# Separate row tiles, single-bank value products and a shorter hand order in the gating and memory attention of a decoder layer

## The chip, the cores and the metric

The kernel runs on one core of a Trainium2 chip. The metric is the device time of one execution in microseconds (us). A core has TensorE (PE in the profile; PEld are its weight loads), VectorE (DVE), ScalarE (ACT), GpSimd (POOL), and SyncE (SP), which issues the DMA transfers. Each engine works through its own queue in order.

## The reference

One layer of a decoder trunk on `x` of 1024 positions by 1024 channels: a half-step SwiGLU, a projection `z` with three gated branches, an output projection, a second half-step SwiGLU. What the change touches are branch A, the chunked spatial gating, and branch C, attention into 256 memory tokens:

```python
z = rmsnorm(x, mix_norm) @ w_in          # columns u, v, c_q, c_kv, k_rope, q_mem, gates
u = gelu(z[..., U]); v = gelu(z[..., V])
# A: 8 chunks of 128 positions, 8 groups of 64 channels
v = layernorm(v, ln_g, ln_b).reshape(B, nc, CHUNK, SG_GROUPS, SG_GROUP_DIM)
mixed = einsum('gts,bcsgd->bctgd', tril(w_s), v) + b_s
y_a = u * mixed.reshape(B, S, SG_WIDTH)
# C: 4 heads of 128, 256 memory tokens
q = rmsnorm(q_mem); kv = rmsnorm(mem, mem_norm) @ w_kv; k = rmsnorm(kv[K]); v = kv[V]
y_c = softmax(q @ k.T * MD ** -0.5) @ v
merged = sum(sigmoid(gate_i) * (y_i @ W_branch_i) for i in A, B, C)
```

## The kernel before, in words

Every product is computed to float32 accuracy from two halves of each operand: `split` (L129 to L131) makes `hi` by a cast on ScalarE (L130) and `lo = x - hi` on VectorE (L131); `split_gain` does the same with a factor (L139, L140); `mm3` (L144 to L150) issues three matmuls, hi·hi (L147), lo·hi or hi·lo (L148, L149). PSUM tiles come from four single banks (`bank`, 512 columns each) and from two tiles of two banks (`mm`).

After the first SwiGLU and the projections, `mixer` (L1005) calls `sgu` (L614), which does branch A's mixing and, in the same stretch, all of the memory attention:

- `take(hf)` for both halves of 512 positions. `gelu_rows` multiplies and applies gelu (L601) to four chunks of 128 positions by 512 channels, into `rows`. VectorE takes the statistics (L643, L644), normalises (L647, L649), and a split gives `v_hi`, `v_lo` (L130, L131). `take(0)` and `take(1)` run parts of `mem_norm`, the norm of the memory rows, between their products.
- `mix(hf)` does eight groups of three matmuls, one group to a bank. ScalarE evicts each group with its bias into `m` (L661). After a `yield` it transposes `m` (L668) and multiplies by `u` (L669), and splits the result.
- In the tile pool of `sgu`, `rows` (L636) and `m` (L656) have the same name "u" and one buffer: both halves' rows and both halves' `m` follow each other in it.
- `mem_kv` makes the memory keys and values. Its first product is followed by `head_norm` (L697 Square, L698 copy, L699 sum) and by mix(0)'s matmuls; in the middle of its second product stand mix(0)'s transposes. Key transposes (L425) follow. `mem_queries` squares the query columns on ScalarE (L784, out of `raw`, in two halves of 64 rows), adds on GpSimd (L787), splits the queries, and sums with a `pick` matrix (L794).
- `branches(0, ...)` is branch A's projection, a generator of steps of 12 matmuls each.
- `mem_attention` interleaves, for eight blocks of 128 queries: `scores` (S: products into an `mm` tile, minimum L816, factor L817, exponentials L821, division L825 and L826), `turn` (T: eight transposes L863 into banks and splits), `value` (V: products for two blocks and a split), and steps of branch A (F). A table in the code gives the sequence.

From `mem_kv` to the end of `mem_attention`, the lines stand in a `manual_schedule` block for TensorE: TensorE issues in the order in which the code is written. Outside such a block the tile framework's scheduler chooses the order of each engine. The other engines are always in the scheduler's order. Afterwards follow branch C's projection (`branch_pairs`), the latent attention B, its projection, the output projection and the second SwiGLU.

Of the kernel before, what the change touches and what calls it, by code (L numbers as in the profile page):

```python
# [8 lines left out]
F32 = mybir.dt.float32  # L9
# [7 lines left out]
P = 128  # L17
# [6 lines left out]
SGW = 512  # L24
# [8 lines left out]
MH = 4  # L33
MD = 128
# [11 lines left out]
class Kernel:  # L46
# [551 lines left out]
    def gelu_rows(self, dst, h, w, pairs, amid={}):  # L598


        gelu = lambda d, x: self.nc.scalar.activation(d, x, ACT.Gelu)  # L601
        ps = [self.mm() for _ in range(2)] if pairs else [self.bank() for _ in range(4)]
        for d in range(DT):
            then = amid[d]() if d in amid else None
            for i in range(4):
                b = ps[i // 2][:, i % 2] if pairs else ps[i]
                first = self.mm3(b, tuple(x[:, i * P:(i + 1) * P] for x in h[d]), w[d], d == 0, d == DT - 1)
                if then:
                    self.after(first, then)
                then = None  # L610
        for i, b in enumerate(ps):
            gelu(dst[:, 2 * i:2 * i + 2] if pairs else dst[:, i], b)

    def sgu(self, h, p, sink):  # L614
        nc, a, tc = self.nc, self.a, self.tc
        v8 = lambda tag, dt=F32R: p.tile([P, 4, SGW], dt, name=tag, tag=tag, bufs=2)
        if True:
            ln_g = self.bcast_row(p, "ln_g", a["sg_ln_g"], SGW)
            ln_b = self.bcast_row(p, "ln_b", a["sg_ln_b"], SGW)
            ws = self.raw().rearrange("p (g t) -> p g t", g=SGG)  # L620
            nc.sync.dma_start(ws, a["sg_w"])
            nc.gpsimd.affine_select(
                out=ws, in_=ws, compare_op=ALU.is_ge, fill=0.0, base=0,
                pattern=[[0, SGG], [1, P]], channel_multiplier=-1,
            )
            whi, wlo = (x.rearrange("p (g t) -> p g t", g=SGG) for x in self.split_pair())
            self.split(whi, wlo, ws)
            mem = self.mem_norm()
            next(mem)
            w = self.load(a["w_v"])  # L630
            vs, yt = [], []

            def take(hf, amid={}):
                vhi, vlo = (v8(n) for n in ("v_hi", "v_lo"))
                vs.append((vhi, vlo))
                rows = p.tile([P, 4, SGW], F32, name="u")  # L636
                self.gelu_rows(rows, h[hf], w, hf == 0, amid)
                for i in range(0, 4, 2):
                    st = self.small.tile([P, 2, 6], F32, name="bn", tag="bn")
                    mv = self.small.tile([P, 2, 2], F32, name="mv", tag="mv")  # L640
                    v = rows[:, i:i + 2]
                    for k in range(2):
                        nc.vector.bn_stats(st[:, k], v[:, k])  # L643
                        nc.vector.bn_aggr(mv[:, k], st[:, k])  # L644
                    r = self.rms(mv[:, :, 1], 2, 1)
                    for k in range(2):
                        nc.vector.scalar_tensor_tensor(  # L647
                            v[:, k], in0=v[:, k], scalar=mv[:, k, 0:1], in1=ln_g, op0=ALU.subtract, op1=ALU.mult)
                        nc.vector.scalar_tensor_tensor(  # L649
                            v[:, k], in0=v[:, k], scalar=r[:, k:k + 1], in1=ln_b, op0=ALU.mult, op1=ALU.add)  # L650
                    self.split(vhi[:, i:i + 2], vlo[:, i:i + 2], v)

            def mix(hf):
                if not yt:
                    yt.extend(self.split_pair() for _ in range(4))
                m, v = p.tile([P, 4, SGW], F32, name="u"), vs[hf]  # L656
                for g in range(SGG):
                    b = self.bank()[:, :4 * SGW // SGG].rearrange("p (c d) -> p c d", c=4)
                    cols = slice(g * SGW // SGG, (g + 1) * SGW // SGG)
                    self.mm3(b, (whi[:, g], wlo[:, g]), tuple(x[:, :, cols] for x in v), True, True)  # L660
                    nc.scalar.activation(m[:, :, cols], b, ACT.Identity, bias=self.sg_b[:, g:g + 1])  # L661
                yield
                for j in range(4):
                    u = self.row()
                    nc.sync.dma_start(u, self.z[ZU + j][:, hf])
                    b = self.bank()
                    for c in range(4):
                        nc.tensor.transpose(b[:, c * P:(c + 1) * P], m[:, c, j * P:(j + 1) * P], self.ident)  # L668
                    nc.vector.tensor_tensor(u, u, b, op=ALU.mult)  # L669
                    self.split(*(t[:, hf * 512:hf * 512 + 512] for t in yt[j]), u)  # L670

            take(0, {7: lambda: next(mem)})
            take(1, {3: lambda: next(mem)})
            m0, m1 = mix(0), mix(1)
            with tc.manual_schedule(engines={mybir.EngineType.PE}):
                kv = self.mem_kv(next(mem), (lambda: next(m0, None), lambda: next(m0, None)))
                rooms = [v8(n).rearrange("p (a b) w -> p a (b w)", a=2) for n in ("v_hi", "v_lo")]
                queries = self.mem_queries([(x[:, 0], x[:, 1]) for x in rooms])
                next(queries)
                next(m1)  # L680
                rooms = [v8(n, F32) for n in ("v_hi", "v_lo")]
                rooms = [x.rearrange("p (a h) (b m) -> p a (h b) m", a=2, b=2)[:, k] for x in rooms for k in range(2)]
                branch = self.branches(0, yt, sink)
                next(branch)
                next(m1, None)
                yc = self.mem_attention(next(queries), rooms, *kv, branch)
        return yc

    def head_norm(self, x, ps):
# [15 lines left out]
    def mem_norm(self):  # L705


        nc, a = self.nc, self.a
        views = lambda n, dt: [t[:, i].rearrange("p (c m) -> p c m", m=ML)[:, c]
                               for t in (self.h4(dt) for _ in range(n)) for i in range(2) for c in range(2)]  # L710
        x4 = [self.x4() for _ in range(2)]
        x = [t[:, i, c * ML:(c + 1) * ML] for t in x4 for i in range(2) for c in range(2)]
        for n, t in enumerate(x4):
            nc.sync.dma_start(
                t.rearrange("p a (b m) -> p (a b) m", b=2), a["mem"][:, 4 * n:4 * n + 4])
        acc = self.row()[:, :2 * ML].rearrange("p (a m) -> p a m", a=2)
        for n, t in enumerate(x4):
            sq = self.x4() if n == 0 else sq2
            nc.scalar.activation(sq, t, ACT.Square)
            if n == 0:  # L720
                first, sq2 = sq, self.x4()
        nc.vector.tensor_tensor(first, first, sq2, op=ALU.add)
        nc.vector.tensor_tensor(acc, first[:, 0].rearrange("p (a m) -> p a m", a=2),
                                first[:, 1].rearrange("p (a m) -> p a m", a=2), op=ALU.add)
        nc.vector.tensor_tensor(acc[:, 0], acc[:, 0], acc[:, 1], op=ALU.add)
        yield
        ss = self.token_sums(acc[:, 0], late=True)
        last = self.final
        r = self.rms(ss, ML // P, D)
        yield last  # L730
        scale = self.norm_scale(r, late=True, bank=lambda: self.mm()[:, 0])
        last = self.final
        hi, lo = views(2, F32R), views(2, F32R)
        for c in range(DT):
            self.norm_put(hi[c], lo[c], x[c], self.g_mem[:, c:c + 1], scale)
        yield last
        yield hi, lo
# [63 lines left out]
    def mem_attention(self, queries, rooms, kt, vv, filler):  # L801
# [35 lines left out]

        def value(i):
            pt = st.pop(i)
            o = self.mm().rearrange("p a (b q) -> p (a b) q", b=2)  # L840
            for hh in range(MH):
                for m in range(2):
                    s = tuple(t[:, m, hh * MD:(hh + 1) * MD] for t in vv)
                    self.mm3(o[:, hh], s, tuple(t[:, hh] for t in pt[m]), m == 0, m == 1)
            for hh in range(MH):
                self.split(*(t[:, 2 * i * P:2 * (i + 1) * P] for t in yt[hh]), o[:, hh])

        S, T, V = scores, turn, value
        F = lambda: next(filler, None)
        yt = [self.split_pair(self.h4) for _ in range(MH)]  # L850
# [1152 lines left out]
```

## Time and profile before

| | us |
|---|---|
| median of 3 runs (2221.55 to 2222.67) | 2222.58 |
| the profiled execution | 2222.69 |
| its span, first to last instruction | 2221.0 |
| TensorE busy | 2180.9 (98%) |
| VectorE busy | 1564.4 (70%) |
| ScalarE busy | 912.7 (41%) |

The profile comes from one execution. Each timeline row has the start, the duration, the engine, the line, the operation, and out<-in by tile names; a bracket at its end tells how long the engine stood idle before it, and whose result ended this. A wait of TensorE for a tile is named after what was last released for it. A matmul's shown duration is longer than the distance to the next start, since they are pipelined; the spacing of starts is what a matmul costs. Window rows give the busy time of each engine within a stretch, and the mean clock that TensorE was granted there (1.00 is full).

The stretch of the change: `take(1)`'s last matmuls end at 1124 us, mix(0) starts at 1135.0, mix(1) at 1166.3, the first turn at 1200.4, and the last value ends at 1256.3.

### The profile page before, as it was taken

What the parts mean: (1) busy time and instruction counts of PE and PEld (TensorE: products, weight loads), DVE (VectorE), ACT (ScalarE), POOL (GpSimd) and SP (SyncE); (2) the same over time, 40 slices, a digit from 0 to 9 for tenths busy, and PEclk for the clock granted to TensorE, in tenths of its full rate; (3) what the DMA queues carried; (4) which work ended last, traced back from release to release, by engine and by line L of the source; (5) the groups of instructions that cost most, each with busy time, mean ns of one, the idle gap of its engine ahead of it and who ended that gap; (6) DMA issues with size and microseconds to landing.
All of it is one profiled execution on the core that took longest, in us unless ns stands there. A gap on an engine that the chain in (4) does not pass through costs nothing. (4 is left out here: it accounts for less than half of the span.)

```text
span 2221.0 us, 27576 instructions
## 1 busy us (share of the span) xinstructions
PE 2180.9 (98%) x10256; PEld 1818.3 (82%) x10256; DVE 1564.4 (70%) x2402; ACT 912.7 (41%) x1507; POOL 249.0 (11%) x252
## 2 busy tenths in 40 slices
PE   9999999999999999999979999999999999999999
PEld 5788888888887888888767889988888888888887
DVE  7966666579888555545887668895886666657884
ACT  5422222243455333344465448843342222224432
POOL 0012111100000000001300131140002121210000
PEclk9999999999999999999989999999999999999999
DMA  4242323484432333331634550085033333328543
GB/s 144 81 147 95 101 101 108 152 308 149 150 109 95 115 104 114 133 102 42 224 105 166 213 209 30 30 286 201 35 104 110 100 114 100 114 99 301 179 128 104
DMA packets 116085, 294.29 MB, mean 133 GB/s; under 512 B 13680, under 2 KB 22000, under 8 KB 115952
## 3 DMA queue, kind: packets, MB, share of 16 engines
q1 hardware_dynamic: 115952, 292.55, 38.4%
q8 instruction: 80, 1.31, 0.2%
q14 instruction: 53, 0.43, 0.1%
HBM read 206.00 MB, written 86.51 MB: 132 GB/s over the span
## 5 line engine op out<-in xcount | busy, mean ns | idle before, releaser
L135 ACT CAST whi<-x 128x1024 fp32r<-128x1024 f32 (+1 forms) x201 | 191.2, 954 | 501.8 <-PE one L148 220.3
L1345 DVE TENSOR_TENSOR t<-t,one 128x512 f32<-128x512 f32 x186 | 127.8, 687 | 243.6 <-PE one L149 242.8
L147 PE MATMUL bank<-h,whi 128*128 128x512 f32 x676 | 263.3, 390 | 0.0
L148 PE MATMUL bank<-h,whi 128*128 128x512 f32 x676 | 263.1, 389 | 0.0
L149 PE MATMUL bank<-h,wlo 128*128 128x512 f32 x676 | 263.0, 389 | 0.0
L136 DVE TENSOR_TENSOR wlo<-x,whi 128x1024 fp32r<-128x1024 f32 (+1 forms) x201 | 239.8, 1195 | 31.7 <-ACT whi L135 31.6
L147 PE MATMUL one<-h,whi 128*128 128x512 f32 x508 | 198.7, 391 | 0.7 <-ACT t L1454 0.7
L149 PE MATMUL one<-h,wlo 128*128 128x512 f32 x508 | 197.7, 389 | 0.0
L148 PE MATMUL one<-h,whi 128*128 128x512 f32 x508 | 197.6, 389 | 0.0
L147 PE MATMUL one<-w,whi 128*128 128x512 f32 x424 | 164.9, 389 | 0.0
L148 PE MATMUL one<-w,whi 128*128 128x512 f32 x424 | 164.9, 389 | 0.0
L149 PE MATMUL one<-w,wlo 128*128 128x512 f32 x424 | 164.9, 389 | 0.0
L130 ACT CAST whi<-w 128x1024 fp32r<-128x1024 f32 (+1 forms) x108 | 95.1, 899 | 145.1 <-PE one L148 62.1
L131 DVE TENSOR_TENSOR wlo<-w,whi 128x1024 fp32r<-128x1024 f32 (+1 forms) x108 | 110.1, 1033 | 62.4 <-ACT whi L130 62.3
L1747 POOL TENSOR_TENSOR raw<-raw 128x512 f32<-128x512 f32 x38 | 63.0, 1658 | 806.5 <-DVE raw L1593 806.5
L149 PEld LDWEIGHTS bank<-h,wlo 128*128 128x128 f32 x676 | 126.9, 188 | 26.4
L148 PEld LDWEIGHTS bank<-h,whi 128*128 128x128 f32 x676 | 126.9, 188 | 26.3
L147 PEld LDWEIGHTS bank<-h,whi 128*128 128x128 f32 x676 | 126.9, 188 | 26.1
L147 PE MATMUL bank<-whi 128*128 128x512 f32 x352 | 136.9, 389 | 0.0
L148 PE MATMUL bank<-wlo,whi 128*128 128x512 f32 x352 | 136.9, 389 | 0.0
L149 PE MATMUL bank<-whi,wlo 128*128 128x512 f32 x352 | 136.9, 389 | 0.0
L147 PEld LDWEIGHTS one<-h,whi 128*128 128x128 f32 x508 | 95.4, 188 | 20.8 <-ACT t L1454 1.1
(391 smaller groups left out, 4900.7 us busy)
## 6 DMA issues: line engine op xcount, KB each, us to landing
x<-in_ffn_w_gu_dram SPq DMA_DIRECT2D x78, 512.0 KB, 5.2
w<-tdt SPq DMA_DIRECT2D x40, 512.0 KB, 4.6
tdb<-raw SPq DMA_DIRECT2D x64, 256.0 KB, 2.1
h<-in_ffn_w_down_dram SPq DMA_DIRECT2D x64, 256.0 KB, 6.0
gate<-raw SPq DMA_DIRECT2D x31, 512.0 KB, 2.6
w<-tdb SPq DMA_DIRECT2D x30, 512.0 KB, 4.5
tdt<-w SPq DMA_DIRECT2D x48, 256.0 KB, 2.1
x<-in_w_gate_dram SPq DMA_DIRECT2D x21, 512.0 KB, 6.0
```

The costliest lines, as they stand in the source:

```text
L130: self.nc.scalar.copy(hi, src)
L131: return (eng or self.nc.vector).tensor_tensor(lo, src, hi.bitcast(F32), op=ALU.subtract)
L135: self.nc.scalar.copy(hi, src)
L136: return lambda: self.nc.vector.tensor_tensor(lo, src, hi.bitcast(F32), op=ALU.subtract)
L147: i = mmul(out, s[0], m[0], start=first, stop=False, **kw)
L148: mmul(out, s[0], m[1], start=False, stop=False, **kw)
L149: self.last = mmul(out, s[1], m[0], start=False, stop=last, **kw)
L1345: return self.nc.vector.tensor_tensor(out, x, y, op=ALU.add)
L1747: sub = lambda d, x, y: (eng or nc.gpsimd).tensor_tensor(d, x, y, op=ALU.subtract)
```

## The change

1. `rows` are two tiles of two chunks each from the pools `h4` (second half) and `x4` (first half). The name "u" is left to `m` alone, still with one buffer.
2. `mem_norm` yields once more behind its two loads, and `sgu` resumes it behind the load of `w_v`.
3. `value` uses two single banks, each for two of the four heads, in place of one `mm` tile, and splits each pair as it is done.
4. The call of `mem_attention` stands behind the `manual_schedule` block, so that TensorE's order from the first scores on is the scheduler's.

```diff
@@ gelu_rows
-            gelu(dst[:, 2 * i:2 * i + 2] if pairs else dst[:, i], b)
+            gelu(dst[i] if pairs else dst[i // 2][:, i % 2], b)
@@ sgu
             next(mem)
             w = self.load(a["w_v"])
+            next(mem)
@@ take
-                rows = p.tile([P, 4, SGW], F32, name="u")
+                rows = [(self.h4 if hf else self.x4)() for _ in range(2)]
...
-                    v = rows[:, i:i + 2]
+                    v = rows[i // 2]
@@ end of sgu
-                yc = self.mem_attention(next(queries), rooms, *kv, branch)
+            yc = self.mem_attention(next(queries), rooms, *kv, branch)
@@ mem_norm
                 t.rearrange("p a (b m) -> p (a b) m", b=2), a["mem"][:, 4 * n:4 * n + 4])
+        yield
@@ value
-            o = self.mm().rearrange("p a (b q) -> p (a b) q", b=2)
-            for hh in range(MH):
-                for m in range(2):
-                    s = tuple(t[:, m, hh * MD:(hh + 1) * MD] for t in vv)
-                    self.mm3(o[:, hh], s, tuple(t[:, hh] for t in pt[m]), m == 0, m == 1)
-            for hh in range(MH):
-                self.split(*(t[:, 2 * i * P:2 * (i + 1) * P] for t in yt[hh]), o[:, hh])
+            for pair in range(MH // 2):
+                o = self.bank().rearrange("p (b q) -> p b q", b=2)
+                for hh in (2 * pair, 2 * pair + 1):
+                    for m in range(2):
+                        s = tuple(t[:, m, hh * MD:(hh + 1) * MD] for t in vv)
+                        self.mm3(o[:, hh % 2], s, tuple(t[:, hh] for t in pt[m]), m == 0, m == 1)
+                for hh in (2 * pair, 2 * pair + 1):
+                    self.split(*(t[:, 2 * i * P:2 * (i + 1) * P] for t in yt[hh]), o[:, hh % 2])
```

Behind `next(mem)` all lines move by one, behind `mem_norm`'s `yield` by two, and behind `value` by three (L661 becomes L662, L784 becomes L786, L863 becomes L866).

ScalarE's queue before, from the gelu of the second half's rows to mix(0)'s evictions (L661): behind the four gelu come two pairs of casts of memory weights, Squares of query columns (L784) and the head norm (L697, L698), the casts of the second half's rows (`v_hi<-u`), and then all eight evictions.

```order
L601 ACTIVATE u<-bank 128x512 x4
L130 CAST whi<-raw 128x512 x4
L784 ACTIVATE wlo<-raw 64x1024
L697 ACTIVATE t<-mm 128x512
L698 COPY h_8948<-mm 128x512
L784 ACTIVATE whi<-raw 64x1024 x2
L784 ACTIVATE wlo<-raw 64x1024
L130 CAST v_hi<-u 128x1024
L784 ACTIVATE wlo<-raw 64x1024
L130 CAST v_hi<-u 128x1024
L661 ACTIVATE u<-bank,c_sg_b 128x4x64 x8
```

The same place in ScalarE's queue with the change (the evictions are L662; `h_8642` and `h_8643` are the rows' tiles), from the last of the head norm on; ahead of it stand the gelu, eight casts of memory weights, a Square and the head norm.

```order
L130 CAST whi<-raw 128x512 x8
L786 ACTIVATE wlo<-raw 64x1024
L699 COPY h_8950<-mm 128x512
L786 ACTIVATE whi<-raw 64x1024
L662 ACTIVATE u<-bank,c_sg_b 128x4x64 x4
L786 ACTIVATE whi<-raw 64x1024
L786 ACTIVATE wlo<-raw 64x1024
L130 CAST v_hi<-h_8642 128x1024
L662 ACTIVATE u<-bank,c_sg_b 128x4x64 x2
L130 CAST v_hi<-h_8643 128x1024
L662 ACTIVATE u<-bank,c_sg_b 128x4x64 x2
```

The first four evictions moved ahead of two Squares and of both casts of the second half's rows; the last four stand between and behind these casts. Eight casts of weights instead of four stand behind the gelu, since the gelu moved up.

TensorE's queue before, behind branch A's first step (`x` by `whi`): mix(1)'s 16 transposes (L668), the query sums with `pick`, and two further steps, of which the first three rows stand here, ahead of the first scores.

```order
L149 MATMUL bank<-x_8979,wlo 128x512
L668 MATMUL bank<-ident,u 128x128 x16
L794 MATMUL bank<-pick,whi 128x2 x16
L147 MATMUL bank<-x_8973,whi 128x512
L148 MATMUL bank<-x_8974,whi 128x512
L149 MATMUL bank<-x_8973,wlo 128x512
```

TensorE's queue with the change, at the last groups of mix(1) (`bank<-v_hi,x`): the scores are the rows into `mm`.

```order
L149 MATMUL bank<-v_hi,x_8420 128x256
L147 MATMUL mm<-h_8833,h_9137 128x256
L148 MATMUL mm<-h_8834,h_9137 128x256
L147 MATMUL mm<-h_8833,h_9137 128x256
L148 MATMUL mm<-h_8834,h_9137 128x256
L147 MATMUL bank<-v_hi,x_8419 128x256
L148 MATMUL bank<-v_lo,x_8419 128x256
L149 MATMUL bank<-v_hi,x_8420 128x256
L147 MATMUL bank<-x_8975,whi 128x512
L148 MATMUL bank<-x_8976,whi 128x512
L149 MATMUL mm<-h_8833,h_9138 128x256 x2
```

The first matmuls of two score blocks moved ahead of mix(1)'s last group and of branch A's first step. The rest of these scores stands within mix(1)'s transposes, `pick` follows, and four branch steps come between it and the first turn. Further on, in place of one `value` behind another step, values stand among scores: here TensorE's queue with the change at the scores of the fifth block, into which the first value (`bank<-whi,h_8835`) has been woven.

```order
L149 MATMUL mm<-h_8833,v_hi 128x256
L147 MATMUL bank<-whi,h_8835 128x256
L147 MATMUL mm<-h_8833,v_lo 128x256
L148 MATMUL mm<-h_8834,v_lo 128x256
L149 MATMUL mm<-h_8833,v_lo 128x256
L148 MATMUL bank<-wlo,h_8835 128x256
L149 MATMUL bank<-whi,h_8836 128x256
```

Before, this value stood behind a branch step and went into a tile of two banks (`mm<-whi,h_8833`). From the last value on, TensorE's order is as it was.

## The prediction

> **What bounds the kernel now.** I read the page first, then the waits of TensorE (PE), then windows and timelines around the largest wait.
>
> ```profile
> span 2221.0 us, 27576 instructions
> PE 2180.9 (98%) x10256; PEld 1818.3 (82%) x10256; DVE 1564.4 (70%) x2402; ACT 912.7 (41%) x1507; POOL 249.0 (11%) x252
> ```
>
> TensorE is busy for 2180.9 of 2221.0 us. The diff changes no matmul, so the whole program has 40.1 us of TensorE idleness to win, plus what a halved clock costs. Where it waits, from the end of the `v` rows to the end of the memory attention (1120 to 1260 us; the columns are the time in all, how often, and the longest):
>
> ```profile
> PE bank L147 <- ACT u L661: 14.3, 2, 13.4
> PE mm L147 <- ACT v_lo L821: 3.2, 1, 3.2
> PE bank L147 <- DVE h L140: 2.2, 1, 2.2
> PE mm L147 <- ACT v_hi L821: 1.2, 1, 1.2
> PE bank L863 <- DVE m_mx L817: 0.8, 1, 0.8
> ```
>
> That is 21.7 us, over half of all the idleness, in 140 us: the change sits where the waiting is. The windows give length, busy time of PE, PEld, DVE, ACT, POOL, then the granted clock, the DMA share and GB/s:
>
> ```profile
> 1120.00:1140.00 20.00, 16.61 (x79) 13.79 (x78) 20.00 (x60) 13.34 (x22) 0.00 (x0) 0.98 0.55 174
> 1140.00:1160.00 20.00, 10.03 (x53) 9.02 (x53) 11.65 (x25) 9.85 (x15) 2.56 (x1) 0.67 0.26 90
> 1167.00:1175.00 8.00, 4.88 (x22) 4.04 (x21) 6.18 (x8) 5.37 (x11) 0.00 (x0) 0.69 0.58 189
> 1200.00:1256.30 56.30, 51.51 (x328) 46.18 (x329) 41.15 (x72) 31.63 (x92) 2.29 (x2) 0.97 0.37 124
> 1238.00:1242.00 4.00, 4.00 (x17) 3.38 (x16) 2.40 (x4) 1.09 (x4) 0.00 (x0) 0.57 0.23 66
> ```
>
> VectorE (DVE) is full, 20.00 of 20, while it normalises the second half's `v` rows, and then has room. The large wait itself, on TensorE:
>
> ```profile
> 1136.33 0.28 PE L149 MATMUL bank<-v_hi,x 128*128 128x256 f32 x1
> 1149.97 0.58 PE L147 MATMUL bank<-v_hi,x 128*128 128x256 f32 x1 [13.36 <-ACT u L661]
> 1152.48 0.41 PE L149 MATMUL bank<-v_hi,x 128*128 128x256 f32 x1
> 1153.54 0.39 PE L147 MATMUL mm<-whi,h 128*128 128x512 f32 x1
> 1153.77 0.39 PE L148 MATMUL mm<-wlo,h 128*128 128x512 f32 x1
> 1158.08 0.39 PE L149 MATMUL mm<-whi,h 128*128 128x512 f32 x1
> ```
>
> mix(0) has four PSUM banks. Its fifth group of three matmuls needs the first eviction at L661. On ScalarE (ACT):
>
> ```profile
> 1132.49 1.14 ACT L130 CAST whi<-raw 128x512 fp32r<-128x512 f32 x2 [0.55 <-PE mm L149]
> 1134.99 1.06 ACT L784 ACTIVATE wlo<-raw 64x1024 f32<-64x1024 f32 x1 [1.35 <-PE mm L148]
> 1135.95 0.58 ACT L697 ACTIVATE t<-mm 128x512 f32<-128x512 f32 x1
> 1137.38 0.57 ACT L698 COPY h<-mm 128x512 f32<-128x512 f32 x1
> 1137.97 2.12 ACT L784 ACTIVATE whi<-raw 64x1024 f32<-64x1024 f32 x2
> 1146.52 1.04 ACT L130 CAST v_hi<-u 128x1024 fp32r<-128x1024 f32 x1
> 1149.44 2.04 ACT L661 ACTIVATE u<-bank,c_sg_b 128x256 f32<-128x256 f32 x5 [1.88 <-DVE v_lo L131]
> ```
>
> The eviction waits for a `v_lo` of the other half, because it writes the buffer that this `v_lo` reads:
>
> ```profile
> 1140.85 4.81 DVE L649 SCALAR_TENSOR_TENSOR u<-u,rs_y,ln_b 128x512 f32<-128x512 f32 x4
> 1148.13 1.22 DVE L131 TENSOR_TENSOR v_lo<-u,v_hi 128x1024 fp32r<-128x1024 f32 x1
> ```
>
> So the wait is one of buffers, and not of data: mix(0) reads only the first half's rows.
>
> **Part 1: rows in tiles of their own.** mix(0)'s evictions now need only their banks and ScalarE's turn. In the new order the first eviction stands behind the casts of the memory weights, one Square of gate columns (L786, formerly L784), the four head-norm operations, and one more Square. At the old times these end at 1137.97 + 1.06 = 1139.0; with 0.4 for the eviction itself (2.04 over 5) it is done at 1139.4. TensorE ran dry at 1149.97 − 13.36 = 1136.6, so the wait is at least 2.8 us. Four casts more than before stand between the gelu and the first Square: 4 × 0.57 = 2.3, which makes 5.1 us. I take 4.8, near the upper end, because the casts' data come through the full VectorE. Saved: 13.36 − 4.8 = **8.6** (8.3 to 10.6).
>
> The clock stays halved for a stretch: twelve matmuls from 1149.97 to 1152.7 take 2.7 us, where the unslowed ones stand 0.12 apart (three groups' starts, below, show the same). I keep that loss of 1.3 us as it is.
>
> What is late next? The transposes at L668 read all eight evictions. The last two now stand behind the cast of the second half's rows that ended at 1146.52 + 1.04 = 1147.6, so they are done near 1148.4; the transposes follow the last matmul of that half (1158.08 + 0.23), so they are due at 1158.3 − 8.6 = 1149.7. The first half of the second product hides this with 1.3 us to spare; without that cover the difference would be paid in full. The second half's `v_lo` still ends at 1149.35, and mix(1), which reads it, now begins at 1166.3 − 8.6 = 1157.7: 8 us of cover. The evictions that moved ahead of Squares and casts find their matmuls long done, so they hold up nothing behind them except by their 0.4 us each.
>
> **Part 2: mix(1).** It lasts from 1166.31 to 1174.95:
>
> ```profile
> 1166.31 0.36 PE L147 MATMUL bank<-v_hi,x 128*128 128x256 f32 x1
> 1166.51 0.28 PE L148 MATMUL bank<-v_lo,x 128*128 128x256 f32 x1
> 1166.63 0.28 PE L149 MATMUL bank<-v_hi,x 128*128 128x256 f32 x1
> 1169.43 0.39 PE L147 MATMUL bank<-v_hi,x 128*128 128x256 f32 x1 [2.16 <-DVE h L140]
> 1172.02 0.58 PE L147 MATMUL bank<-v_hi,x 128*128 128x256 f32 x1 [0.92 <-ACT u L661]
> 1174.95 0.63 PE L147 MATMUL bank<-x,whi 128*128 128x512 f32 x1
> ```
>
> 24 matmuls at 0.12 are 2.9 us of its 8.6; waits are 3.1, and the rest is clock. These waits follow from TensorE's own key transposes (ScalarE and VectorE split the keys), so they move with it and stay. But the last group no longer stands alone at the end: the first matmuls of two score tiles come ahead of it and fill its wait. I take **1.6**, half of the idle 3.1; the bounds are 0 and 5.7 (all that is above the matmuls). The two queries' splits, which these scores read, become an early need; ScalarE has 5.37 of 8 us there, and I cost it at nothing, with the 0 as the end if it isn't.
>
> [...]
>
> **Part 3: scores, turns and values in the scheduler's order; values in single banks.** The first turn no longer waits 0.8 for its scores, since four branch steps stand between; **0.8**. From there to the last value were 56 us (the window from 1200 to 1256.3), with waits of 1.2 and 3.2 for a score tile's exponentials (values took the same two-bank tiles as scores), and a clock of 0.57 over 4.0 us, which is 1.7 lost. All that together is 6.1. With values in banks the scores have both tiles to themselves, and these two waits go. In their place turns and values share four single banks, and values follow more closely on the turns' splits:
>
> ```profile
> 1197.88 1.19 DVE L816 TENSOR_REDUCE m_mx<-mm 128x4 f32<-128x1024 f32 x1
> 1198.99 1.21 DVE L826 TENSOR_TENSOR v_hi<-v_hi,m_rs 128x1024 f32<-128x1024 f32 x1
> 1205.15 1.28 DVE L131 TENSOR_TENSOR wlo<-bank,whi 128x512 fp32r<-128x512 f32 x2
> 1197.10 0.56 ACT L821 ACTIVATE v_hi<-mm,m_mx,mq_nr 128x256 f32<-128x256 f32 x1
> ```
>
> One pair of splits is 1.28. Exposed in three of the four rounds, that is 3.8, so 6.1 − 3.8 = 2.3; I take **2.0**. Bounds: +6.1 if nothing is exposed, and if every round waits for both a reduction and a pair of splits, 4 × 2.5 = 10, so −3.9.
>
> **The rest at nothing.** `mem_norm`'s extra yield moves no row beside the casts; its loads land long before use. The four loads of memory weights and three of gate columns (512 KB, 3.6 us each) go in the old sequence on SyncE's queue, as the DMA share of 0.55 and 0.26 allows; a load that slipped a place would cost up to its 3.6. SyncE swaps some stores and loads of gates and branch weights by a place; no wait of TensorE for a transfer is in the list above, so I cost that at nothing too:
>
> ```profile
> raw<-in_mem_w_kv_dram SPq DMA_DIRECT2D x4, 512.0 KB, 3.6
> raw<-gate SPq DMA_DIRECT2D x3, 512.0 KB, 3.6
> ```
>
> GpSimd's one operation in 1140 to 1160 (2.56 us) feeds the query sums, which are read after mix(1). After the last value all orders are the old ones, shifted.
>
> **Sum.** 8.6 + 1.6 + 0.8 + 2.0 = 13.0. The profiled execution took 2222.7 (span 2221.0 and 1.7 around it), 0.1 above the median, so 2222.7 − 13.0 = **2209.7**.
>
> **Rivals.**
>
> *The wait goes whole.* If ScalarE reached the first eviction as TensorE runs dry, the gap and its slow clock would go: 13.4 + 1.3, with mix(1)'s 5.7 and the tail's 2.8 some 23 us, 2199.7. Against it stands the three-microsecond chain of Squares and head norm in ScalarE's order. For it: nothing but that order keeps the eviction back.
>
> *The debt stays.* VectorE is full through 1140 and TensorE may only meet its debt later: at L668 or in mix(1), with a wait as long as the one removed, or the rows' new tiles wait for older readers in their pools and the change doesn't separate anything in time. Then 2222. Against it: 11.65 of 20 us of VectorE in 1140 to 1160, with the data that TensorE wants next done at 1149.35, and in ScalarE's new order the gelu of neither half stands later than it stood.
>
> *The scheduler's order exposes the softmax (slower).* A turn needs reduction 1.2, four exponentials of 0.56, scaling 1.2, and a little scalar work: about 5.0 us from the scores. If in each of the four rounds of the tail a turn or value reaches the head of TensorE's queue that long before its data, 20 us are added; TensorE runs in order, so all branch steps behind it wait too. With the other parts' 11.0 that gives 2222.7 − 11.0 + 20 = 2231.7. It decides once each round loses over 2.75 us. For it: the hand order had placed a branch step behind each score, and that order is given up. Against it: the new order still has branch steps or other scores between a score and its turn, and a branch step takes 12 × 0.23 = 2.7 us (the spacing of 512-wide matmuls at 1153.54).
>
> **How the numbers follow.** Forecast and its neighbours, 0.74; the whole wait gone 0.10; the debt stays 0.08; exposed softmax 0.08. The low bounds sum to 8.3 + 0 + 0 − 3.9 = 4.4 (2218.3), the high ones to 10.6 + 5.7 + 0.8 + 6.1 = 23.2 (2199.5). I take 2200 to 2218.5, which leaves the two unfavourable rivals out, and a part of the first. A measurement of this kernel can tell about 0.2%, 4.4 us, from no change. Faster by more than that 0.84, within it 0.08, slower 0.08.
>
> **What would show it.** Right: the first L662 on ScalarE begins near 1141, on TensorE the 13.4 is a wait of 3 to 5 us for the same line, L668 has none, and no wait for L821's exponentials is on a score tile. The chosen 1.6 and 2.0 are the weakest; from mix(1)'s start to the last value the 90.0 us (1166.3 to 1256.3) should have become about 85.6. Wrong: a new wait for the cast or the `v_lo` of the second half's rows at L669, or for turns' splits in every round, of over 2 us each.

## The result, and the profile after

The changed kernel takes 2208.89 us (median; 2208.37 to 2209.34 in 4 runs), the kernel before 2222.11 beside it: 13.2 us less, a ratio of 0.994 with a 95% interval of 0.9923 to 0.9958. The forecast was 2209.7.

The page of the changed kernel, its first two lines:

```profile
span 2206.9 us, 27578 instructions
PE 2177.5 (99%) x10256; PEld 1816.0 (82%) x10256; DVE 1564.4 (71%) x2402; ACT 912.1 (41%) x1507; POOL 249.4 (11%) x252
```

VectorE's and ScalarE's busy time and all counts of matmuls are as before; what went is TensorE's idleness, 40.1 to 29.4 us, and some slow clock. TensorE's waits in the changed stretch (1100 to 1260 us):

```profile
PE bank L147 <- ACT u L662: 5.0, 1, 5.0
PE bank L147 <- DVE h L140: 2.5, 1, 2.5
PE bank L147 <- DVE wlo L131: 1.0, 1, 1.0
PE bank L866 <- DVE wlo L131: 0.9, 1, 0.9
PE bank L866 <- DVE t L1022: 0.5, 1, 0.5
PE bank L147 <- DVE h L131: 0.4, 1, 0.4
```

That is 10.3 us for 21.7. The first wait is the one of 13.4; both waits for exponentials (`v_hi`, `v_lo` of L821) and the first turn's 0.8 are gone, and four waits of 0.4 to 1.0 have come in their place. TensorE's timeline at the places where the steps begin:

```profile
1133.38 0.28 PE L147 MATMUL bank<-v_hi,x 128*128 128x256 f32 x1
1139.93 0.58 PE L147 MATMUL bank<-v_hi,x 128*128 128x256 f32 x1 [4.96 <-ACT u L662]
1142.66 0.63 PE L147 MATMUL mm<-whi,h 128*128 128x512 f32 x1
1148.64 1.91 PE L669 MATMUL bank<-ident,u 128*128 128x128 f32 x16
1156.63 0.36 PE L147 MATMUL bank<-v_hi,x 128*128 128x256 f32 x1
1160.10 0.39 PE L147 MATMUL bank<-v_hi,x 128*128 128x256 f32 x1 [2.51 <-DVE h L140]
1164.62 0.40 PE L147 MATMUL bank<-x,whi 128*128 128x512 f32 x1
1189.21 1.03 PE L866 MATMUL bank<-ident,v_hi 128*128 128x128 f32 x8
1242.28 0.40 PE L147 MATMUL bank<-x,whi 128*128 128x512 f32 x1
```

In order: mix(0), its fifth group, the second product, mix(0)'s transposes (with no wait), mix(1), its wait, branch A's first step, the first turn, and the step behind the last value. From mix(0) to the second product it was 17.68 us before (1135.01 to 1152.69) and is 9.28 now. ScalarE shows why 5 us are left:

```profile
1132.90 1.14 ACT L130 CAST whi<-raw 128x512 fp32r<-128x512 f32 x2 [3.44 <-DMA raw<-in_mem_w_kv_dram]
1135.48 1.05 ACT L786 ACTIVATE wlo<-raw 64x1024 f32<-64x1024 f32 x1 [1.44 <-DMA raw<-gate]
1138.46 1.06 ACT L786 ACTIVATE whi<-raw 64x1024 f32<-64x1024 f32 x1
1139.43 1.53 ACT L662 ACTIVATE u<-bank,c_sg_b 128x256 f32<-128x256 f32 x4
```

The first eviction stands behind a cast and a Square that each waited for a load (3.44 and 1.44 us), and behind the head norm. The clock, in windows (columns as before):

```profile
1140.00:1143.00 3.00, 3.00 (x13) 3.00 (x14) 2.79 (x10) 2.96 (x5) 0.00 (x0) 0.50 0.99 386
1157.00:1165.00 8.00, 5.45 (x29) 5.00 (x29) 6.66 (x6) 7.07 (x14) 1.30 (x1) 0.79 0.24 86
1175.55:1181.24 5.69, 5.69 (x14) 4.44 (x15) 3.33 (x16) 2.54 (x5) 0.31 (x1) 0.50 0.34 109
1188.00:1242.30 54.30, 51.46 (x336) 45.89 (x335) 40.41 (x69) 29.68 (x85) 2.00 (x2) 1.00 0.44 142
```

It still halves behind mix(0)'s wait (0.50), falls less in mix(1) (0.79 for 0.69), and stays full in the memory attention's tail (1.00). It is also at 0.50, for 5.7 us (3.1 before), behind the query sums with `pick`, where TensorE waits for nothing (busy for all of the 5.69 us).

In the runs below, stretches are read from TensorE's timeline: M0 (mix(0) begins), P2 (second product), M1 (mix(1)), F1 (first step of branch A), T0 (first turn), C (first matmul of branch C's projection). In us:

| | M0-P2 | P2-M1 | M1-F1 | F1-T0 | T0-C | M0-C | median | ratio to before (95%) |
|---|---|---|---|---|---|---|---|---|
| before | 17.68 | 13.62 | 8.64 | 25.40 | 64.17 | 129.5 | 2222.11 | |
| changed | 9.28 | 13.97 | 7.99 | 24.59 | 61.26 | 117.1 | 2208.89 | 0.9940 (0.9923 to 0.9958) |
| 1 rows alone | 9.95 | 13.78 | 7.83 | 25.59 | 62.60 | 119.8 | 2214.86 | 0.9962 (0.9950 to 0.9975) |
| 2 rows, banks | 9.82 | 14.11 | 7.24 | 26.99 | 60.86 | 119.0 | 2211.39 | 0.9947 (0.9933 to 0.9961) |
| 3 rows, order | 7.08 | 14.89 | 8.03 | 23.26 | 60.39 | 113.7 | 2209.58 | 0.9938 (0.9926 to 0.9951) |
| 4 changed, mix(0) split | 1.43 | 18.42 | 12.11 | 24.88 | 61.27 | 118.1 | 2211.65 | 0.9951 (0.9938 to 0.9963) |
| 5 banks alone | 16.69 | 14.38 | 8.28 | 25.97 | 60.84 | 126.2 | 2220.45 | 0.9989 (0.9980 to 0.9998) |
| 6 order alone | 17.48 | 13.71 | 9.05 | 24.38 | 59.06 | 123.7 | 2217.51 | 0.9977 (0.9968 to 0.9986) |
| 7 banks, order | 16.69 | 14.37 | 9.09 | 24.68 | 60.93 | 125.8 | 2219.87 | 0.9985 (0.9976 to 0.9994) |
| 8 run 2, additions moved | 9.69 | 13.84 | 6.60 | 26.54 | 60.84 | 117.5 | 2210.31 | 0.9944 (0.9931 to 0.9956) |
| 9 run 3, additions moved | 9.50 | 13.98 | 7.45 | 22.82 | 61.31 | 115.1 | 2208.59 | 0.9940 (0.9927 to 0.9952) |
| 10 run 4, additions moved | 1.43 | 18.10 | 11.83 | 22.44 | 61.30 | 115.1 | 2209.00 | 0.9939 (0.9925 to 0.9952) |
| 11 changed, early load | 7.16 | 13.71 | 8.20 | 24.56 | 61.25 | 114.9 | 2207.74 | 0.9934 (0.9922 to 0.9947) |
| 12 run 9, early load | 7.16 | 13.64 | 7.72 | 22.76 | 61.27 | 112.6 | 2207.97 | 0.9933 (0.9920 to 0.9947) |

The stretches come from one execution each, the medians from several; the two need not differ by the same amount. In run 3's profile mix(0) begins 3.1 us later than in run 2's (1137.64 and 1134.57); a granted clock of 0.91 between 1080 and 1100 us makes 1.8 us of this, and the other engines worked on meanwhile (VectorE for 18.2 of these 20 us), so its short M0-P2 is in part that. Runs 5 and 7 begin mix(0) late in their profiles too (1137.52 and 1137.64); why is not shown. Run 1's profile is of its fastest execution (2212.13 us), run 2's and run 7's are of their slowest. So the medians' order counts, and the stretches say where.

### The profile page after: what moved, and what is told of

It reads as the page before. It is cut to its first block, busy times and chain, and to the rows that moved or that the text cites. A ratio compares the mean times of both kernels' runs of the same rounds, so it can differ in the third digit from the quotient of the medians.

```text
span 2206.9 us, 27578 instructions
## 1 busy us (share of the span) xinstructions
PE 2177.5 (99%) x10256; PEld 1816.0 (82%) x10256; DVE 1564.4 (71%) x2402; ACT 912.1 (41%) x1507; POOL 249.4 (11%) x252
## 4 chain that ended last, share of the span: by engine, by line
PE 88%; DVE 7%; ACT 2%; DMA 1%; issue 1%; SPq 0%; POOL 0%; ACTq 0%; DVEq 0%; POOLq 0%
PE one L147 14%; PE one L148 14%; PE one L149 14%; PE bank L147 13%; PE bank L148 12%; PE bank L149 12%; PE mm L147 1%; PE mm L148 1%; PE mm L149 1%; PE bank L948 1%; PE bank L963 1%; PE bank L964 1%; DVE wlo L136 1%; DVE wlo L131 1%; PE bank L425 1%
```

## The experiments

**1. Rows alone.** The kernel before, with only the first part of the change (its main line; two more follow from it):

```diff
-                rows = p.tile([P, 4, SGW], F32, name="u")
+                rows = [(self.h4 if hf else self.x4)() for _ in range(2)]
```

> The kernel before, with the rows in tiles of their own and nothing else of the change. Theory one (the 13.4 us were a wait for a buffer): TensorE's wait in mix(0) falls to about 5 us, the clock phase gives up to 0.5 more, and the tail of the memory attention keeps its waits of 1.2 and 3.2 us: 2222.1 - 8.8 = 2213.3 us. Rival (VectorE's debt, which only the new order of the scores fills): the wait comes back in mix(1) or at the transposes of mix(0), and the time is 2218 to 2222 us.

2214.86 us. TensorE's waits in this run:

```profile
PE bank L147 <- ACT u L661: 5.6, 1, 5.6
PE mm L147 <- ACT v_lo L821: 3.2, 1, 3.2
PE bank L147 <- DVE h L140: 2.9, 1, 2.9
```

Theory one holds: 13.4 became 5.6, and the wait did not come back at the transposes or in mix(1) (2.9 for 2.2). Alone, this edit gives 7.9 of the 13.2 us, against 8.8 expected. The tail's waits of 3.2 and 1.2 stand as before, and yet T0-C is 1.6 us shorter (62.60 for 64.17). That is the clock: behind the same two waits it stayed full here, in the window that had 0.96 in the kernel before:

```profile
1200.00:1245.00 45.00, 40.58 (x267) 36.55 (x266) 34.00 (x59) 24.71 (x72) 2.29 (x2) 1.00 0.36 120
```

**2. Rows and banks, hand order kept.**

```diff
-            yc = self.mem_attention(next(queries), rooms, *kv, branch)
+                yc = self.mem_attention(next(queries), rooms, *kv, branch)
```

> The changed kernel with the call of the memory attention back under the hand order: rows of their own and single-bank values, without the scheduler's order. Theory one (the single banks remove the tail's waits, since scores no longer queue behind a value for a tile): 2222.1 - 8.8 - 2.5 = 2210.8 us, and no wait of TensorE for L821's exponentials. Rival (the scheduler's order is what fills the waits): within 1 us of rows alone, 2213 us, with waits of 2 us and more for turns' splits in the tail.

2211.39 us, as theory one had it. The waits of the tail that are new beside run 1:

```profile
PE bank L147 <- DVE wlo L131: 1.7, 1, 1.7
PE bank L148 <- DVE wlo L131: 0.8, 2, 0.6
```

The waits for exponentials (1.2 and 3.2) are gone with the order untouched; turns' splits cost 1.7 and 0.8. From the first turn on that is 4.4 − 2.5 = 1.9, and T0-C fell by 62.60 − 60.86 = 1.7.

**3. Rows and order, values in two banks.** The changed kernel with `value` as it was (the first line shown).

```diff
-                o = self.bank().rearrange("p (b q) -> p b q", b=2)
+            o = self.mm().rearrange("p a (b q) -> p (a b) q", b=2)
```

> The changed kernel with the values in a tile of two banks as before: rows of their own and the scheduler's order. Theory one (banks): values take a score's tile again, TensorE waits for exponentials 2 to 4 us in all, 2211 to 2213 us. Rival (order): the scheduler knows of the shared tiles and places other work there, so 2209 to 2210 us, as the whole change.

2209.58 us: the rival. Its waits:

```profile
PE bank L147 <- ACT u L662: 3.8, 1, 3.8
PE bank L147 <- DVE h L140: 2.8, 1, 2.8
PE mm L147 <- DVE h L131: 1.1, 1, 1.1
PE bank L149 <- DVE wlo L131: 0.4, 1, 0.4
PE bank L865 <- DVE wlo L131: 0.2, 1, 0.2
```

The scheduler places the scores so that sharing tiles with the values costs 1.1, and no wait for exponentials is left in this order (run 9 shows another). With the order free, the single banks bring nothing that can be measured (0.9938 and 0.9940).

**4. mix(0) split around the second product.** The remaining wait is given other work:

```diff
+                    if g == 4 and not hf:
+                        yield
...
-                kv = self.mem_kv(next(mem), (lambda: next(m0, None), lambda: next(m0, None)))
+                kv = self.mem_kv(next(mem), [lambda: next(m0, None)] * 3)
...
         ps = product(w, amid[1])
+        amid[2]()
```

> The changed kernel, with mix(0)'s last four groups moved into the middle of the second product of the memory keys and values, and its transposes behind that product: the 4.96 us wait finds 24 matmuls (5.4 us) in its place. If ScalarE's order alone makes that wait: the wait and its halved clock go, 5 to 6 us, 2203.5 us. If VectorE's debt stands behind it: the wait goes, but the wait of mix(1) for the split keys (2.5 us) grows to 4 to 5, so the net is 3 us, 2206 us. I hold the second for likelier. If the time doesn't move, the debt is whole: 2209 us.

2211.65 us, so none of the 5 us was kept; "the debt is whole" was the closest, and what I held likelier was wrong. M0 to F1 is 1.43 + 18.42 + 12.11 = 32.0 us against 31.2 in the changed kernel. The waits moved:

```profile
PE bank L147 <- ACT u L664: 3.1, 1, 3.1
PE bank L425 <- DVE t L672: 2.1, 1, 2.1
```

ScalarE and SyncE in this run, three rows and one:

```profile
1149.05 1.57 ACT L664 ACTIVATE u<-bank,c_sg_b 128x256 f32<-128x256 f32 x4
1150.49 1.16 ACT L139 ACTIVATE v_hi<-raw,m_gq 128x1024 fp32r<-128x1024 f32 x1
1160.08 1.15 ACT L139 ACTIVATE v_lo<-raw,m_gq 128x1024 fp32r<-128x1024 f32 x1
```

```profile
1153.00 0.32 SPq L786 DMA_DIRECT2D raw<-gate  x1
```

Counted from the start of mix(0), the late evictions hold back the split of a query (15.5 us for 13.1 in the changed kernel), this its load buffer, and this the next load of query columns (18.0 us for 16.8); mix(1)'s evictions stand on ScalarE behind the splits that need this load. The transposes of mix(0), now behind the second product, add the 2.1 us ahead of the key transposes. So, as these rows read, TensorE's wait is one end of a chain through load buffers, ScalarE and VectorE, and filling it did not shorten the chain.

**5. Banks alone**, on the kernel before (run 3's diff the other way).

> The kernel before with single-bank values alone: rows and evictions share their buffer, hand order kept. With rows apart, the banks took 1.7 us off the stretch from the first turn to branch C (62.6 to 60.9 us). If the tail's gain is its own, it is the same here: 2222.5 - 1.7 = 2220.8 us, with the 13.4 us wait of mix(0) as it was. Rival (VectorE sets the tail's end, so banks pay only when the rows come apart): 2222.5 us.

2220.45 us; the first theory. T0-C is 60.84, as with the rows apart (60.86), so this gain is the tail's own; mix(0)'s wait was 12.4, in a profile in which mix(0) began 2.5 us later than in the kernel before.

**6. Order alone**, on the kernel before (run 2's diff the other way).

> The kernel before with the hand order ended at the first scores, and nothing else. If the order is worth the same with and without rows apart: the values in two banks with that order were 5 us below rows alone (2209.6 against 2214.9), of which half were clock, so 2222.5 - 4 = 2218.5 us. Rival (the free order only makes up for what the shared buffer delays): over 5 us, under 2217. Second rival (exposed softmax): over 2222.5.

2217.51 us, between the first two numbers: about 5 us, and no exposed softmax. The waits behind the first turn in this run are

```profile
PE mm L147 <- DVE h L131: 1.1, 1, 1.1
PE bank L863 <- DVE wlo L131: 0.2, 1, 0.2
```

in place of the hand order's 4.4. The slow clock behind the longer of them is gone too (1.00 for 0.96 between 1200 and 1245 us), as it was in run 1 with the waits in place.

**7. Banks and order, rows in the shared buffer.** The changed kernel with the first diff undone.

> The changed kernel with the rows back in the buffer that the evictions use: single banks and the scheduler's order. If banks and order do the same work twice, as the runs with rows apart suggest, it is within 1.5 us of the order alone: 2218.5 us, and TensorE waits 13 us in mix(0). If they add up: 2217 us or less.

2219.87 us, 2.4 above the order alone, where the expectation gave 1.5: banks and order don't add up here. On top of the order, the banks rather cost: the tail's waits are 1.3, 0.9, 0.5 and 0.4 us for 1.1 and 0.2, and T0-C is 60.93 for 59.06. The intervals of 6 and 7 overlap, so that the banks harm is not shown; that they don't help is.

**8. The query additions moved to VectorE**, in run 2:

```diff
-            nc.gpsimd.tensor_tensor(sq[0], sq[0], sq[1], op=ALU.add)
+            nc.vector.tensor_tensor(sq[0], sq[0], sq[1], op=ALU.add)
```

> The changed kernel with the hand order kept (2211.4 us), and GpSimd's two additions of query squares moved to VectorE. Beside these additions VectorE's operations were longer: the head norm's scaling 3.3 us and a query split 2.3 us, against 1.2 and 1.3 elsewhere. If the additions cause that, the two return to 1.2 and 1.3, 3.1 us less, against two additions of 1.2: VectorE gains 0.7, and the first branch step comes up to that much earlier, so 2210.7 us, within the scatter of 2211.4. Rival (the two are long for their own operands): they stay at 3.3 and 2.3, VectorE has 2.4 us more to do, 2213.8 us.

2210.31 us, as the first theory says, and within the scatter. First VectorE and GpSimd in the changed kernel, then VectorE in this run:

```profile
1143.36 3.32 DVE L704 TENSOR_TENSOR h<-h,rs_y 128x1024 f32<-128x1024 f32 x1
1157.06 2.32 DVE L140 SCALAR_TENSOR_TENSOR v_lo<-raw,m_gq,v_lo 128x1024 fp32r<-128x1024 f32 x1 [2.12 <-ACT v_lo L139]
```

```profile
1143.18 2.41 POOL L789 TENSOR_TENSOR whi<-whi,wlo 128x1024 f32<-128x1024 f32 x1 [43.86 <-ACT wlo L786]
1155.93 2.37 POOL L789 TENSOR_TENSOR whi<-whi,wlo 128x1024 f32<-128x1024 f32 x1 [10.34 <-ACT wlo L786]
```

```profile
1143.74 1.23 DVE L789 TENSOR_TENSOR whi<-whi,wlo 128x1024 f32<-128x1024 f32 x1 [0.50 <-ACT wlo L786]
1147.83 1.22 DVE L704 TENSOR_TENSOR h<-h,rs_y 128x1024 f32<-128x1024 f32 x1
1158.04 1.28 DVE L140 SCALAR_TENSOR_TENSOR v_lo<-raw,m_gq,v_lo 128x1024 fp32r<-128x1024 f32 x1
```

Without GpSimd beside them, the two take 1.22 and 1.28 us for 3.32 and 2.32. The same addition, 2.56 us, ran beside the old kernel's L649, whose four operations took 4.81 us, against 2.73 in the changed kernel, where GpSimd is idle beside them. On VectorE it costs 1.23 us, less than the 2.1 us by which it lengthened L704. The two engines worked side by side for 2.2 us at L704 and for 1.2 us at L140, and VectorE's operations became 2.1 and 1.0 us longer, nearly as much as that. By what they hinder each other is not shown.

**9. The same in run 3.**

> The changed kernel with values in two-bank tiles, as in the third experiment (2209.6 us), and the query additions on VectorE. It would be the fastest so far if the 1.1 us that the additions gave under the hand order are to be had here too: 2208.5 us. Rival (the scheduler's new order of scores undoes it): 2209.6 us or more.

2208.59 us, and 0.9940: not to be told from run 3 or from the changed kernel. The scheduler's order is another here, and with the values in two-bank tiles 2.5 us of waits for exponentials are back:

```profile
PE mm L147 <- ACT v_hi L823: 1.5, 1, 1.5
PE mm L147 <- ACT v_lo L823: 1.0, 1, 1.0
```

**10. The same in run 4.**

> The split mix(0) of the fourth experiment (2211.7 us) with the query additions on VectorE. If what gave the split's gain back is the chain of query loads and splits through VectorE, which GpSimd's additions lengthen by 2.1 and 1.0 us, mix(1) is shorter by 1 to 2 us, 2210 us. Rival (the chain is set by ScalarE's order and the load buffers): 2211.7 us, mix(1) still some 12 us long.

2209.00 us, but not for the reason expected: mix(1) is 11.83 us long (12.11), as the rival says; what got shorter is F1-T0, 24.88 to 22.44. So the chain of run 4 is not VectorE's speed there. F1-T0 has the same matmuls in both runs. From the first `pick` matmul to the first branch matmul that is again followed at 0.23 to 0.24 us, run 4 takes 9.60 us with 12 branch matmuls between (1174.03 to 1183.63), run 10 takes 7.56 us with 10 (1173.57 to 1181.13). Less 0.46 for the two, that makes 1.6 of the 2.4 us, and a wait of 0.4 us is gone. Run 9 has 7.45 us with 10 there. What made the slow stretch shorter is not shown.

**11. The layer norm's rows loaded early.**

```diff
-            ln_g = self.bcast_row(p, "ln_g", a["sg_ln_g"], SGW)
-            ln_b = self.bcast_row(p, "ln_b", a["sg_ln_b"], SGW)
+            ln_g, ln_b = self.ln
...
+        lnp = rows.enter_context(tc.tile_pool(name="ln", bufs=1))
+        self.ln = [self.bcast_row(lnp, n, a["sg_" + n], SGW) for n in ("ln_g", "ln_b")]
         with tc.tile_pool(name="lt", bufs=1) as self.lp:
```

> The changed kernel with the layer norm's gain and bias rows loaded at the start of the mixer instead of at 1103 us; the order of TensorE, ScalarE and GpSimd is the same. In the changed kernel VectorE stood idle for 3.80 us at 1107 for this load, and was then full until 1138. If VectorE's debt is what the rest of the waits hang on: it works that off up to 3.8 us earlier, the wait in mix(0) falls from 5.0 to 2 to 3 us, and the first branch step comes 2 to 4 us earlier: 2206 us. Rival (ScalarE's order and the loads of weights set the first eviction): the wait stays at 5, 2208.9 us.

2207.74 us. What it aims at is this row of VectorE in the changed kernel:

```profile
1107.24 1.41 DVE L648 SCALAR_TENSOR_TENSOR x<-x,mv,ln_g 128x512 f32<-128x512 f32 x2 [3.80 <-DMA ln_g<-in_sg_ln_g_dram]
```

And the waits of TensorE in this run:

```profile
PE bank L147 <- DVE h L140: 3.1, 1, 3.1
PE bank L147 <- ACT u L661: 2.8, 1, 2.8
```

mix(0)'s wait fell from 5.0 to 2.8, by a load that TensorE never waits for, and M0-C by 2.2. The last of the four loads of memory weights is issued as VectorE frees a load buffer with a split (`wlo<-raw`), here in the changed kernel and in this run:

```profile
1129.62 0.33 SPq L96 DMA_DIRECT2D raw<-in_mem_w_kv_dram  x1
```

```profile
1126.73 0.33 SPq L96 DMA_DIRECT2D raw<-in_mem_w_kv_dram  x1
```

That is 3.8 us ahead of mix(0) in the changed kernel and 7.2 us in this run (7.3 in the kernel before), and ScalarE's waits of 3.44 and 1.44 us for loads are gone. So of the remaining wait 2.2 us were VectorE's backlog, passed on by the weights' load buffers. The profile's 2.2 stands against medians 1.2 apart, with overlapping intervals; the place of the gain is shown, the gain over the whole program isn't settled.

**12. The same in run 9.**

> The same early load in the version of the ninth experiment (values in two-bank tiles, query additions on VectorE; 2208.6 us). With VectorE's debt as the cause the gains add: 2205.5 us, below both kernels. Rival as before: 2208.6 us.

2207.97 us and not 2205.5: no better than run 11 by the medians, though its stretch M0-C is the shortest (112.6 us). That the gains add is not shown. Runs 11 and 12 lie below the changed kernel by about 1 us, less than can be told.

## Why the prediction was right, point by point

- **mix(0).** Forecast: a wait of 4.8, 8.6 saved. Measured: 4.96, and 17.68 − 9.28 = 8.4. Run 1 shows that the rows' tiles do it. The place in ScalarE's queue was right, the working of the size in part luck. The 2.3 us for four more casts are not what was paid: run 11 has the same casts in the same places and a wait of 2.8, the lower bound of the forecast. What was paid in their stead are 2.2 us for the late last load of weights; the forecast had costed the loads at nothing. Its remark that the casts' data come through the full VectorE points at the right engine, which delays this load. The transposes, which were to have 1.3 us to spare, had no wait.
- **P2 to mix(1)**, costed at nothing, took 0.35 more: the slow clock reached into the second product (a matmul of 0.63 us at 1142.66, for 0.39 before).
- **mix(1) and the first turn.** Forecast 1.6 + 0.8 = 2.4. Measured 1.5 (M1 to T0: 34.0 to 32.6). This is the term that was mis-sized. The wait for the split keys stayed, as said (2.5 for 2.2); the scores' first matmuls filled the 0.9 and not half of the idle. And the clock over F1-T0 was 0.86 for 0.89, 3.4 us lost for 2.8, for which the forecast had no term.
- **The tail.** Forecast 2.0, from 6.1 gone and 3.8 exposed in new waits. Measured 2.9 from the first turn to the end of the last value (55.9 to 53.0); the new waits were 1.0 + 0.9 + 0.5 + 0.4 = 2.8. Of the 6.1, the 1.7 of slow clock went in run 1 too, with nothing in the tail changed, so they are no effect of the banks or the order. The errors here and in mix(1) are 0.9 us each, with opposite signs; it is luck that the stretch from mix(1) to the last value came to 85.65 us (1156.63 to 1242.28) for the forecast 85.6.
- **mem_norm's yield at nothing.** Compiled with and without it, all five engines have the same operations in the same order, only some load buffers differ; no run timed it alone.
- **The sum.** M0 to C fell by 12.4 us. The two profiles differ by 14.1; 1.6 of this lies ahead of the change (the first product of memory keys begins at 1124.13 and 1122.50), where the kernels do the same.

The rivals: the wait didn't go whole; softmax wasn't exposed, with the order alone (run 6) or in the changed kernel. The debt was no bar to this change, but it is there behind it: run 4 took the next wait away by order, and got it back in mix(1). And the parts are not independent. The single banks and the free order each remove the same 4.4 us of waits for exponentials (runs 2 and 5, 3 and 6), and together no more (run 7); the order alone does so only as the scheduler happens to lay it (run 9). The rows alone give 7.9 us, and taking them out of the changed kernel costs some 11.

## What to carry to other kernels

A wait that ends with another product's reader can be a wait for a buffer, as mix(0)'s 13.4 us were (5.6 in run 1): name the tile that both use, and give one of them its own. Two edits that remove the same waits need not add up (the 4.4 us of runs 5 to 7 did not), so try each without the other. Before filling a wait with other work, follow the chain of loads, casts and evictions behind it; run 4 filled one and gained nothing, and run 11 shortened one by a load 30 us ahead.

## What the runs showed of the hardware

- The length of a wait did not settle here whether TensorE's clock fell behind it. In the changed kernel a wait of 2.5 us was followed by a clock of 0.62 (1160.10 to 1164.62), the tail's 2.8 us in pieces by 1.00. The same wait of 3.2 us was followed by 0.57 over 4 us in the kernel before and by 1.00 in run 1.
- The clock fell without a wait, too: in the changed kernel 32 `pick` matmuls of two columns each, 4.0 us of them, were followed by 5.7 us at 0.50. What decides when is not shown.
- Run 3's five executions scatter with the clock: they lie between 2206.60 us at a mean clock of 0.997 and 2210.54 at 0.994.
- An addition on GpSimd of 2.4 us lengthened one VectorE operation, beside it for 2.2 us, by 2.1 us (3.32 for 1.22 in run 8), and another, beside it for 1.2 us, by 1.0 us (2.32 for 1.28).
